# Winograd pairs of the up-projection: three PSUM tiles for one pair, weight sums loaded earlier, cache copies moved to the gate panels, residual updates at high priority

## The chip, the core and the metric

The kernel runs on one core of a Trainium2 chip. Such a core has five engines that run side by side, each through its own queue in program order: TensorE (PE in the profile; its weight loads are shown apart as PEld), VectorE (DVE), ScalarE (ACT), GpSimd (POOL) and SyncE (SP). Matmuls write to PSUM, which has eight banks of 2 KB per partition; the other data lies in SBUF. DMA transfers are issued by SyncE and, where they add to what lies in SBUF or copy from DRAM to DRAM, by GpSimd. Engines wait for each other through semaphores. The metric is the device time of one execution in microseconds.

## The reference

One layer of a hybrid decoder for 512 prompt tokens and 8 sample tokens, 520 columns in all, of width 1024. What this document speaks of comes behind the two attentions:

```
u = rmsnorm(x);  qA..gB = split(u @ w_in)
oA = dilated window attention;  oB = gated linear attention
mix = sigmoid(gA) * (oA @ w_pa) + sigmoid(gB) * (oB @ w_pb)
h = x + mix @ w_o
y = h + square(relu(rmsnorm(h) @ w_up)) @ w_down      # w_up 1024 x 4096
```

The sample group's key and value caches are copied to the outputs as well, some 40 MB.

## The kernel before

**Numbers.** Everything is fp32. Each operand is split into a high part (rounded to the matmul's fp32r format) and the rest, and a product takes three matmuls: high x high, high x low, low x high. The activations are kept transposed, 128 rows of the width by 520 columns (two halves of 260); `hh`/`hl` are the two parts of the residual times the norm's weight, `fh`/`fl` those of the squared Relu, `whi`/`wlo` those of the weights.

**Panels.** The weights come as a list of panels of 128 output columns (eight tiles of 128 x 128, 512 KB): 16 gate panels (`gA`, `gB`) end the input projection, then 2 for w_pa, 8 for w_pb, 8 for w_o, and four quarters of the feed-forward part. A plain panel (`panel_mm`) is 48 matmuls. SyncE loads panels two ahead into three rotating buffers (`raw`); ScalarE makes `whi` and VectorE `wlo` (`split_piece`, L107 and L108), half a panel at a time, for small panels in four rotating pairs of buffers.

**Pairs.** In the first three quarters two panels of w_up are done together (`pair_mm`, L185) in Winograd's form of a 2 x 2 block product, with seven products of 4 x 3 = 12 matmuls, where plain panels take eight. The three accumulators are x, e and a. P1 goes to x; ScalarE copies x to a (L1091); P5 goes to e; P6 is added to x, P3 to e, P7 to x, P2 to a, P4 to x. In between ScalarE and VectorE take copies and sums of what stands there (`up_pair`). a and e are the two banks of one PSUM tile, x is a bank of a second pool with four. At a pair's end come Relu, square and the split into `fh`/`fl`, which the eight panels of w_down then use; the fourth quarter uses plain panels.

**Sums.** Of the activations, the kernel forms `tr`, `Th`, `Tl` from the scaled residual `hg` (`column_sums`, L1064 to L1072), one k tile behind the residual update. Of the weights, `load_pair` loads the second panel into a tile `sums` (SyncE), and then GpSimd issues a DMA that adds parts of both panels onto it (L96); VectorE adds two more times (`s`, L122 and L123). There are three buffers for `sums`. A pair's loads are issued two panels ahead.

**Order.** The queues are filled by a scheduler that simulates the program and takes what is ready by priority; `high_priority` puts instructions ahead of others. `behind` fixes an order between two instructions of a queue, and all panel loads are chained so. `pace(1)` issues one of 42 copies of the caches (1 MB each) from GpSimd, behind the last matmul issued; before, it was called once per panel of w_pb, w_o and the feed-forward part, and once per pair.

Of the kernel before, what the change touches and what calls it, by code (L numbers as in the profile page):

```python
# [9 lines left out]
F32 = mybir.dt.float32  # L10
# [3 lines left out]
ALU = mybir.AluOpType  # L14
# [11 lines left out]
KT = 8  # L26
# [4 lines left out]
AHEAD = 4  # L31

# [15 lines left out]
class Build:  # L48
# [42 lines left out]
    def load_pair(self, i):  # L91

        ap, p = self.panels[i][0], self.late
        sums = p.tile([P, KT, P], F32, tag="sums", name="sums", bufs=3)
        self.load(sums, ap[1])
        self.nc.gpsimd.dma_start(sums.rearrange("p (i k) n -> p i (k n)", i=2),  # L96
                                 ap[:, :, :4].rearrange("i p k n -> p i (k n)"), accum_op=ALU.add)
        ra = self.raw_tile(KT)
        self.load(ra, ap[0])
        rb = p.tile([P, 4, P], F32, tag="rb", name="rb", bufs=2)  # L100
        self.load(rb, ap[1][:, 4:])
        self.raw[i] = (ra, rb, sums)
# [12 lines left out]
    def pair_pieces(self, i):  # L115
# [7 lines left out]
        nc.vector.tensor_tensor(s[:, 4:], s[:, :4], ra[:, 4:], op=ALU.add)  # L123
        both = self.split_piece(s, 0, KT)
# [3 lines left out]
        yield self.split_piece(ra, 4, 4)  # L128
# [36 lines left out]
    def start_panels(self, panels):  # L165
        self.panels, self.raw, self.split, self.wdst, self.cur, self.pieces = panels, {}, {}, {}, 0, {}
        self.jobs, self.ready = {}, {}

    def pair_mm(self, acts, done):
# [3 lines left out]
        ae, x = self.pm.tile([P, 2, 512], F32, tag="m", name="mps"), self.bank("mps")[:, :HC]  # L173
        a, e = (ae[:, j, :HC] for j in range(2))
        for q, (n, o, fresh) in enumerate((("P1", x, True), ("P5", e, True), ("P6", x, False), ("P3", e, False),
                                           ("P7", x, False), ("P2", a, False), ("P4", x, False))):
# [12 lines left out]
            done(n, ae, x)  # L189
# [5 lines left out]
    def panel_mms(self, xh, xl, m, pool=None):  # L195
# [3 lines left out]
        self.cur += 1  # L199
        if i + 2 < len(self.panels):  # L200
            self.load_panel(i + 2)
# [872 lines left out]
    def up_pair(self, p, work, k, fh, fl):  # L1074
# [12 lines left out]
        def done(n, ae, x):  # L1087
            a, e = (ae[:, j, :HC] for j in range(2))
# [9 lines left out]
            elif n == "P3":  # L1098
                nc.vector.tensor_tensor(e, e, v["P6"], op=ALU.add)
# [4 lines left out]
            elif n == "P2":  # L1104
                f = work()
# [3 lines left out]
                nc.scalar.activation(v["t"][:, two], v["t"][:, two], AF.Relu, scale=-1.0)  # L1109
            else:  # L1110
                t = v["t"]
# [457 lines left out]
```

## Time and profile before

| what | us |
|---|---|
| median of 3 runs (918.6 to 919.86) | 918.89 |
| the profiled execution | 918.5 |
| its span in the trace | 916.7 |
| w_o panels end, first pair starts | 528.87 |
| last pair ends, w_down of the third quarter starts | 768 |

The page's second part cuts the span into 40 slices of 22.9 us. The busy share of TensorE and VectorE is given in tenths, with the clock granted to TensorE in tenths of full speed and the mean busy share of the DMA engines:

```profile
PE   9999999999999999999999979999999999999996
DVE  6866656865868678677655666635763575556644
PEclk9999999999999999999999979999999999999999
DMA  7576465325543642221887984589658962222402
```

TensorE is full but for one slice (504 to 527 is the 23rd, 527 to 550 the 24th) and the end. The same slice has a lower clock. The DMA engines are busiest from the 20th slice (435 us) on and nearly free in the three slices ahead of it, where the gate panels run.

In the list of waits each row names who waited for whom, with the total in us, how often, and the longest. In the chain each row is a start, a duration and what ran; the chain follows what ended last back to the start. In the order of time a row's bracket gives the idle time ahead of it and what ended that. In the rows by stretch come the stretch, the busy us of PE, PEld, DVE, ACT and POOL (number of instructions), the granted clock, the DMA share and GB/s.

### The profile page before, as it was taken

How to read it: one execution, taken by the hardware profiler on the slowest of the kernel's cores; microseconds unless marked ns; L12 is line 12 of the kernel's file. 1: busy time of each engine (PE TensorE's matmuls, PEld its weight loads, DVE VectorE, ACT ScalarE, POOL GpSimd, SP SyncE). 2: the span in 40 equal slices, each digit the busy share in tenths (PEclk: the TensorE clock that was granted, in tenths of full speed). 3: DMA queues.
4: the chain of work that ended last, by engine and by line, in shares of the span. 5: the costliest groups of instructions: out<-in, count | busy, mean ns of one | idle time of the engine just before them, and what ended most of it. 6: DMA issues, size and time to landing. Idle time of an engine off the chain costs nothing.

```text
span 916.7 us, 19479 instructions
## 1 busy us (share of the span) xinstructions
PE 889.3 (97%) x8010; PEld 868.3 (95%) x8010; DVE 595.0 (65%) x1167; ACT 412.8 (45%) x832; POOL 87.7 (10%) x139
## 2 busy tenths in 40 slices
PE   9999999999999999999999979999999999999996
PEld 9999999999999999999999968899999999999996
DVE  6866656865868678677655666635763575556644
ACT  6334333444545453547334446623752374223442
POOL 1200000000111212010000210011001100000000
PEclk9999999999999999999999979999999999999999
DMA  7576465325543642221887984589658962222402
GB/s 250 157 236 208 139 204 192 117 74 166 183 155 128 208 166 72 76 93 53 310 311 275 304 260 150 207 280 349 221 212 295 359 192 93 93 93 91 140 7 88
DMA packets 42721, 165.16 MB, mean 180 GB/s; under 512 B 5692, under 2 KB 10820, under 8 KB 40808
## 3 DMA queue, kind: packets, MB, share of 16 engines
q1 hardware_dynamic: 33976, 97.93, 30.9%
q0 software_dynamic: 8368, 65.49, 21.2%
q8 instruction: 63, 1.03, 0.4%
q10 hardware_dynamic: 288, 0.49, 0.2%
q14 instruction: 26, 0.21, 0.1%
HBM read 150.17 MB, written 54.17 MB: 223 GB/s over the span
## 4 chain that ended last, share of the span: by engine, by line
PE 90%; ACT 4%; DMA 3%; DVE 2%; issue 1%; SPq 0%; DVEq 0%; ACTq 0%; POOLq 0%
PE mps L220 64%; PE mps L185 10%; PE mps L1384 5%; DMA sums<-in_w_up 2%; ACT whi L107 1%; PE mps L384 1%; PE lev L813 1%; PE sps L559 1%; PE pvp L592 1%; PE gpo L922 1%; PE gpu L926 1%; PE ptp L576 1%; PE vps L523 1%; PE gpo L924 1%; PE gso L994 0%
## 5 line engine op out<-in xcount | busy, mean ns | idle before, releaser
L107 ACT ACTIVATE whi<-raw 128x512 fp32r<-128x512 f32 (+1 forms) x242 | 149.6, 622 | 298.0 <-PE mps L220 247.0
L220 PE MATMUL mps<-uh,whi 128*128 128x260 f32 x896 | 255.8, 286 | 0.0
L220 PE MATMUL mps<-ul,whi 128*128 128x260 f32 x896 | 255.7, 285 | 0.0
L220 PE MATMUL mps<-uh,wlo 128*128 128x260 f32 x896 | 255.2, 285 | 0.0
L108 DVE TENSOR_TENSOR wlo<-raw,whi 128x512 fp32r<-128x512 f32 (+1 forms) x242 | 163.9, 680 | 75.5 <-ACT whi L107 73.2
L220 PEld LDWEIGHTS mps<-uh,wlo 128*128 128x128 f32 x896 | 168.7, 188 | 2.1 <-issue 1.3
L220 PEld LDWEIGHTS mps<-ul,whi 128*128 128x128 f32 x896 | 168.6, 188 | 1.2 <-issue 0.3
L220 PEld LDWEIGHTS mps<-uh,whi 128*128 128x128 f32 x896 | 168.7, 188 | 1.1 <-issue 0.7
L220 PE MATMUL mps<-fl,whi 128*128 128x260 f32 x384 | 108.2, 282 | 0.6 <-DVE fl L1085 0.6
L220 PE MATMUL mps<-fh,wlo 128*128 128x260 f32 x384 | 108.5, 283 | 0.0
L220 PE MATMUL mps<-fh,whi 128*128 128x260 f32 x384 | 108.5, 283 | 0.0
L220 PEld LDWEIGHTS mps<-fl,whi 128*128 128x128 f32 x384 | 72.2, 188 | 0.8 <-DVE fl L1085 0.8
L220 PEld LDWEIGHTS mps<-fh,whi 128*128 128x128 f32 x384 | 72.3, 188 | 0.0
L220 PEld LDWEIGHTS mps<-fh,wlo 128*128 128x128 f32 x384 | 72.2, 188 | 0.0
L185 PE MATMUL mps<-Th,whi 128*128 128x260 f32 x192 | 56.7, 295 | 15.6 <-ACT mps L1091 11.5
L185 PE MATMUL mps<-Tl,whi 128*128 128x260 f32 x192 | 55.4, 288 | 1.6 <-DVE Tl L1072 1.6
L185 PE MATMUL mps<-Th,wlo 128*128 128x260 f32 x192 | 54.9, 286 | 0.0
L185 PEld LDWEIGHTS mps<-Th,whi 128*128 128x128 f32 x192 | 36.8, 192 | 18.7 <-ACT mps L1091 14.2
L1384 PE MATMUL mps<-fh,lw 128*128 128x280 f32 (+1 forms) x256 | 46.8, 284 | 0.0
L185 PE MATMUL mps<-hl,whi 128*128 128x260 f32 x144 | 41.2, 286 | 0.0
L185 PE MATMUL mps<-hh,whi 128*128 128x260 f32 x144 | 41.2, 286 | 0.0
L185 PE MATMUL mps<-hh,wlo 128*128 128x260 f32 x144 | 41.1, 286 | 0.0
(381 smaller groups left out, 1921.1 us busy)
## 6 DMA issues: line engine op xcount, KB each, us to landing
raw<-in_w_in SPq DMA_DIRECT2D x55, 512.0 KB, 4.4
raw<-in_w_down SPq DMA_DIRECT2D x32, 512.0 KB, 3.3
raw<-in_w_up SPq DMA_DIRECT2D x20, 512.0 KB, 7.5
sums<-in_w_up SPq DMA_DIRECT2D x12, 512.0 KB, 8.8
sums<-in_w_up POOLq DMA_DIRECT2D x12, 512.0 KB, 9.7
sx<-in_state SPq DMA_DIRECT2D x8, 512.0 KB, 4.4
sx<-dV SPq DMA_DIRECT2D x8, 512.0 KB, 4.8
out_sgla<-sx POOLq DMA_DIRECT2D x8, 512.0 KB, 5.1
```

The source lines that it names most:

```text
L107: self.piece = (nc.scalar.activation(hi, raw[:, x:x + n], AF.Copy), nc.vector.tensor_tensor(lo, raw[:, x:x + n], hi.bitcast(F32), op=ALU.s ...
L108: nc.vector.tensor_tensor(lo, raw[:, x:x + n], hi.bitcast(F32), op=ALU.subtract))
L185: mm = nc.tensor.matmul(o, w[:, k], u, start=(fresh and k == 0 and y == 0), stop=(k == 3 and y == 2), skip_group_check=True)
L220: mm = self.nc.tensor.matmul(o[:, :HC], wt, x[:, k, j * HC:(j + 1) * HC], start=(k == 0 and n == 0), stop=(k == kt - 1 and n == 2))
L384: self.last = nc.tensor.matmul(ps[i][:, j, :HC], wt, u[:, k, j * HC:(j + 1) * HC], start=(k == 0 and n == 0), stop=(k == KT - 1 and n == 1))
L523: nc.tensor.transpose(pt[:, r * P:(r + 1) * P], vt[:, r * P:(r + 1) * P], self.c["ident"])
L559: m = nc.tensor.matmul(pss[hh][:, hp, c], Q[rows, i, b * P:(b + 1) * P], K[rows, i, ks], start=True, stop=True)
L576: nc.tensor.transpose(pt[:, hh, x], prs[hp][:, hh, x * P:(x + 1) * P], self.c["ident"])
L592: m = nc.tensor.matmul(po[64 * hh:64 * hh + 64, hp * P:(hp + 1) * P], v, pTs[hp][:, hh, x], start=(x == first), stop=(x == 1))
L813: m = self.nc.tensor.matmul(out, w, x, start=True, stop=True)
L922: nc.tensor.matmul(po[:, :256], ST[:, c], V[:, c], start=True, stop=(c == 0))
L1384: nc.tensor.matmul(ps, w, u[:, kk, cc], start=(kk == 0 and x == 0), stop=(kk == KT - 1 and x == 2))
```

## The change

Six edits:

- `pair_mm`: e is a tile of its own in the first pool, a and x are two banks of the second. P3's sum on VectorE goes to a work tile in SBUF instead of back to e, so that Relu on ScalarE handles a alone (260 columns) and the square on VectorE takes max(f, 0) x f.
- `load_sums`: the two DMAs of `sums` are issued up to 22 us of panel time ahead (10.04 per pair, 5.74 per panel), the raw parts of a pair as before.
- In the first pair, P2 is moved from the sixth to the third place and its weights are split earlier.
- `proj_scaled` issues one cache copy per gate panel, 16 in all; so the copies end in the first quarter's w_down instead of the third's.
- The residual update (`H`, `hh`, `hl`) is at high priority.
- `column_sums` of a k tile comes right behind its residual update.

```diff
+LEAD = 22.0
...
     def load_pair(self, i):
-        ap, p = self.panels[i][0], self.late
-        sums = p.tile([P, KT, P], F32, tag="sums", name="sums", bufs=3)
-        self.load(sums, ap[1])
-        self.nc.gpsimd.dma_start(sums.rearrange("p (i k) n -> p i (k n)", i=2),
-                                 ap[:, :, :4].rearrange("i p k n -> p i (k n)"), accum_op=ALU.add)
...
-        self.raw[i] = (ra, rb, sums)
+        self.raw[i] = (ra, rb, self.sums.pop(i))
+
+    def load_sums(self, i):
+        for j in range(i, len(self.panels)):
+            if self.at[j] - self.at[i] > LEAD:
+                return
+            if self.panels[j][1] == PAIR and j not in self.begun:
+                self.begun.add(j)
+                ap = self.panels[j][0]
+                self.sums[j] = t = self.late.tile([P, KT, P], F32, tag="sums", name="sums", bufs=3)
+                self.load(t, ap[1])
+                self.nc.gpsimd.dma_start(t.rearrange("p (i k) n -> p i (k n)", i=2),
+                                         ap[:, :, :4].rearrange("i p k n -> p i (k n)"), accum_op=ALU.add)
...
     def pair_mm(self, acts, done):
-        ae, x = self.pm.tile([P, 2, 512], F32, tag="m", name="mps"), self.bank("mps")[:, :HC]
-        a, e = (ae[:, j, :HC] for j in range(2))
+        self.load_sums(i)
+        e = self.pm.tile([P, 2, 512], F32, tag="m", name="mps")[:, 0, :HC]
+        a, x = (self.bank("mps")[:, :HC] for _ in range(2))
...
+        if i == self.first_pair:
+            seq.insert(2, seq.pop(5))
...
     def panel_mms(self, xh, xl, m, pool=None):
+        if self.late is not None:
+            self.load_sums(i)
...
-    def proj_scaled(self, dst):
+    def proj_scaled(self, dst, copies=0):
...
             self.fill(self.rate)
+            self.pace(copies)
...
             elif n == "P3":
-                nc.vector.tensor_tensor(e, e, v["P6"], op=ALU.add)
+                v["f"] = work()
+                nc.vector.tensor_tensor(v["f"][:, two], e, v["P6"], op=ALU.add)
...
-                nc.scalar.activation(halves(f), ae[:, :, :HC], AF.Relu)
-                nc.vector.tensor_tensor(f, f, f, op=ALU.mult)
+                nc.scalar.activation(f[:, one], a, AF.Relu)
+                nc.vector.scalar_tensor_tensor(f, f, 0.0, f, op0=ALU.max, op1=ALU.mult)
...
+                with tc.high_priority():
+                    nc.vector.tensor_tensor(halves(H[:, k]), ps, halves(H[:, k]), op=ALU.add)
...
-                if k > 0:
-                    self.column_sums(p, hg, k - 1, Th, Tl)
+                self.column_sums(p, hg, k, Th, Tl)
                 self.pace(1)
-            self.column_sums(p, hg, KT - 1, Th, Tl)
```

What stands in the queues moves with it. On SyncE, from the third w_o panel's load to the second pair's loads, before:

```order
L81 DMA raw<-in_w_o 128x1024 x6
L81 DMA sums<-in_w_up 128x1024
L81 DMA raw<-in_w_up 128x1024
L81 DMA rb<-in_w_up 128x512
L81 DMA sums<-in_w_up 128x1024
```

and in the changed program:

```order
L82 DMA raw<-in_w_o 128x1024 x5
L82 DMA sums<-in_w_up 128x1024
L82 DMA raw<-in_w_o 128x1024
L82 DMA sums<-in_w_up 128x1024
L82 DMA raw<-in_w_up 128x1024
L82 DMA rb<-in_w_up 128x512
```

The first `sums` has moved ahead of the last w_o panel's load, and the second ahead of the first pair's own panels.

On VectorE, beside the fifth to seventh w_o panel, behind the residual part `hl` of the fifth, before:

```order
L1302 SCALAR_TENSOR_TENSOR hl<-H,gcols,hh 128x520
L1067 TENSOR_TENSOR tr<-hg 128x260
L1068 SCALAR_TENSOR_TENSOR tr<-tr,hg 128x260
L1069 SCALAR_TENSOR_TENSOR tr<-tr,hg 128x260
L108 TENSOR_TENSOR wlo<-raw,whi 128x512
L1072 TENSOR_TENSOR Tl<-tr,Th 128x780
L122 TENSOR_TENSOR s<-sums,raw 128x512
L1300 TENSOR_TENSOR H<-mps,H 128x520
```

and in the changed program:

```order
L1327 SCALAR_TENSOR_TENSOR hl<-H,gcols,hh 128x520
L1088 TENSOR_TENSOR tr<-hg 128x260
L1089 SCALAR_TENSOR_TENSOR tr<-tr,hg 128x260
L132 TENSOR_TENSOR s<-sums,raw 128x512
L118 TENSOR_TENSOR wlo<-raw,whi 128x512
L1090 SCALAR_TENSOR_TENSOR tr<-tr,hg 128x260
L133 TENSOR_TENSOR s<-s,raw 128x512
L1325 TENSOR_TENSOR H<-mps,H 128x520
```

`s`, which waits for the sums, has moved ahead of `wlo`, the first half of the seventh w_o panel's weights.

On ScalarE, at the end of the second quarter's first pair, before (`t<-t 128x520` is the square of the pair's second output, `mps<-mps` the copy of x to a in the next pair):

```order
L1106 ACTIVATE t<-mps 128x520
L107 ACTIVATE whi<-raw 128x512
L1112 ACTIVATE t<-mps 128x260
L1113 ACTIVATE t<-t 128x520
L107 ACTIVATE whi<-rb 128x512
L1091 ACTIVATE mps<-mps 128x260
L1084 ACTIVATE fh<-t 128x520 x2
```

and in the changed program:

```order
L1129 ACTIVATE t<-mps 128x260
L117 ACTIVATE whi<-raw 128x512
L1135 ACTIVATE t<-mps 128x260
L1105 ACTIVATE fh<-t 128x520
L1136 ACTIVATE t<-t 128x520
L117 ACTIVATE whi<-rb 128x512
L1111 ACTIVATE mps<-mps 128x260
L1105 ACTIVATE fh<-t 128x520
```

One of the two `fh`, that of the pair's first output, has moved ahead of the copy.

More of the change, by code (lines that the diff above doesn't have):

```diff
@@ L166, in start_panels @@
         self.panels, self.raw, self.split, self.wdst, self.cur, self.pieces = panels, {}, {}, {}, 0, {}
-        self.jobs, self.ready = {}, {}
+        self.jobs, self.ready, self.sums, self.begun = {}, {}, {}, set()
+        self.at = np.cumsum([0.0] + [10.04 if p[1] == PAIR else 5.74 for p in panels])
     def pair_mm(self, acts, done):
@@ L188, in pair_mm @@
                     self.last = mm
-            done(n, ae, x)
+            done(n, a, e, x)
     def panel_mm(self, xh, xl, pool=None):
@@ L1085, in split, with done @@
             nc.vector.tensor_tensor(fl[:, k + x], f, fh[:, k + x].bitcast(F32), op=ALU.subtract)
-        def done(n, ae, x):
-            a, e = (ae[:, j, :HC] for j in range(2))
+        def done(n, a, e, x):
             if n == "P1":
@@ L1134, in run @@
         order += [(I["w_o"][i], KT) for i in range(8)]
+        self.first_pair = len(order)
         for qd in range(4):
```

32 lines of the change are left out of this document (19 added, 13 removed).

## The prediction

> **What bounds the kernel now.** I read the page's busy table first, then the waits of TensorE, then the chain, and last the order of time on each engine around the places where TensorE stops.
>
> ```profile
> span 916.7 us, 19479 instructions
> PE 889.3 (97%) x8010; PEld 868.3 (95%) x8010; DVE 595.0 (65%) x1167; ACT 412.8 (45%) x832; POOL 87.7 (10%) x139
> 768.15 91.84 PE mps L220 x768
> ```
>
> TensorE is the bound: it is idle for 916.7 - 889.3 = 27.4 us only. The third row is a stretch of the chain without a wait: 768 matmuls of 260 columns in 91.84 us, 0.1196 us each. That pitch is the measure for everything below: a plain panel of 48 matmuls should take 5.74 us, a pair of 84 (seven products of 12) 10.05 us. No edit takes a matmul away, so only idle time and slow clock can be won.
>
> ```profile
> PE mps L185 <- ACT mps L1091: 11.5, 12, 1.3
> PE mps L185 <- ACT Th L1071: 4.0, 2, 3.6
> PE mps L185 <- DVE Tl L1072: 1.6, 2, 1.2
> PE mps L220 <- DVE fl L1085: 0.6, 1, 0.6
> DVE s L122 <- DMA sums<-in_w_up: 16.9, 4, 5.7
>   issue: 4.1, 3
> ```
>
> These are waits: total us, how often, the longest. Four of them stop TensorE, all inside the pairs (L185) or right behind them; the rest of the idle time lies at the two ends of the program, which the change doesn't touch. The first is product P5 of each of the 12 pairs, which waits for ScalarE's copy of P1. The fifth row is VectorE, blocked on the weight sums that the second and third rows go back to; the last, from the view of the tile s, is idle time of VectorE ahead of s, 4.1 us more, for which the profile shows no releaser.
>
> **The change part by part.** *Separate tiles for a, e and x.* The restarts of P5, from the chain:
>
> ```profile
> 553.05 7.35 PE mps L185 x59
> 564.30 7.35 PE mps L185 x59
> 575.91 7.35 PE mps L185 x59
> 656.45 7.34 PE mps L185 x59
> 668.08 8.88 PE mps L185 x72
> ```
>
> From restart to restart a pair takes 11.25 us (564.30 - 553.05) or 11.6 us (575.91 - 564.30, 668.08 - 656.45). Against 10.05 us that is 1.19 or 1.57 us lost. Of the eleven pairs after the first, four are of the long kind (restarts at 553.05, 575.91, 668.08 and the last) and seven short: 4 x 1.57 + 7 x 1.19 = 14.6 us. In one of them the four small matmuls of the norm hide (about 0.5 us), so 14.1 us can go. With a tile of its own P5 needs nothing from the copy; P6 does, as it goes on in the bank that the copy reads. P5 covers 12 x 0.1196 = 1.44 us. What is late next is therefore the copy itself, behind what stands ahead of it on ScalarE:
>
> ```profile
> 550.79 0.37 ACT L1112 ACTIVATE t<-mps 128x260 f32<-128x260 f32 x1
> 551.05 0.63 ACT L1084 ACTIVATE fh<-t 128x520 fp32r<-128x520 f32 x1
> 551.59 0.62 ACT L1113 ACTIVATE t<-t 128x520 f32<-128x520 f32 x1
> 552.11 0.61 ACT L107 ACTIVATE whi<-rb 128x512 fp32r<-128x512 f32 x1
> 552.63 0.37 ACT L1091 ACTIVATE mps<-mps 128x260 f32<-128x260 f32 x1
> 550.17 0.28 PE L185 MATMUL mps<-hh,whi 128*128 128x260 f32 x1
> ```
>
> This is a long one: with fh ahead of it the copy ends 553.00 - 550.17 = 2.83 us behind the pair's first matmul, and P6 would want to start after 2 x 1.44 = 2.87 us. The changed order puts fh ahead of the copy in nearly every pair, so nearly all look like this one: just covered, with 0.04 us to spare. But fh waits for VectorE's square, and on VectorE a weight split (0.69 us, as s below) may stand ahead of that. I let a part of it through, 0.05 to 0.25 us, and take **0.12 us per pair, 1.3 us** in all; bounds 0 and, if the whole 0.69 less the 0.04 shows in some nine pairs, 6 us.
>
> *The half-width Relu and the fused max.* ScalarE's Relu goes from 520 to 260 columns, VectorE's square becomes a two-operation form (0.76 us, as hl below, for 0.69). Both lie beside TensorE: ScalarE is 45% and VectorE 65% busy. Nothing, between -0.1 and +0.1 us a pair, inside the 0.12 above.
>
> *Sums loaded earlier, residual at highest priority, P2 drawn ahead: the first pair.*
>
> ```profile
> 528.87 0.28 PE L185 MATMUL mps<-hh,whi 128*128 128x260 f32 x1
> 537.44 0.58 PE L185 MATMUL mps<-Th,whi 128*128 128x260 f32 x1 [3.63 <-ACT Th L1071]
> 514.95 0.43 DVE L1069 SCALAR_TENSOR_TENSOR tr<-tr,hg 128x260 f32<-128x260 f32 x1
> 520.78 0.69 DVE L122 TENSOR_TENSOR s<-sums,raw 128x512 f32<-128x512 f32 x1 [3.51 <-DMA sums<-in_w_up]
> 531.41 0.69 DVE L122 TENSOR_TENSOR s<-sums,raw 128x512 f32<-128x512 f32 x1 [2.60 <-DMA sums<-in_w_up]
> 534.57 0.70 DVE L1300 TENSOR_TENSOR H<-mps,H 128x520 f32<-128x520 f32 x1
> 536.71 0.76 DVE L1302 SCALAR_TENSOR_TENSOR hl<-H,gcols,hh 128x520 fp32r<-128x520 f32 x1
> 540.42 0.97 DVE L1072 TENSOR_TENSOR Tl<-tr,Th 128x780 fp32r<-128x780 f32 x1 [0.32 <-ACT Th L1071]
> 540.00:545.00 5.00, 4.16 (x18) 3.85 (x18) 1.12 (x3) 1.11 (x3) 0.50 (x1) 0.50 0.72 242
> ```
>
> The first pair runs from 528.87 to 550.17 (quoted above), 21.30 us, **11.25 over**: 1.1 us for the copy, 5.6 us of waits for Th and Tl (4.0 + 1.6 in the table above), and 4.5 us for the rest. In the last row, a stretch of 5 us, the third number from the end is the granted clock, 0.50: these 5 us alone lose 2.5, so I put the clock at 3 us and the restarts behind the waits at 1.5. VectorE stood still 3.51 and 2.60 us for the sums, so the last residual panel, finished on TensorE at 528.87, was added only at 534.57. From there to the end of the last Tl it took 541.39 - 534.57 = 6.8 us. If nothing blocks, that addition starts near 529.1, and Tl ends near 535.9; the changed order has two more weight splits in between (0.6 us apart), so 535.9 to 537.2. P6, now fourth, reaches its last quarter at 528.87 + 3 x 1.44 + 10 x 0.12 = 534.4. That leaves 1.5 to 2.8 us of waiting, plus 0.3 us for P2 behind the copy.
>
> Do the sums come early enough?
>
> ```profile
> 502.07 3.17 SPq L81 DMA_DIRECT2D sums<-in_w_up  x1
> 507.44 0.33 SPq L81 DMA_DIRECT2D raw<-in_w_up  x1
> 509.99 1.28 POOL L96 DMA_DIRECT2D sums<-in_w_up  x1 [3.14 <-ACT Th L1071]
> sums<-in_w_up POOLq DMA_DIRECT2D x1, 512.0 KB, 10.8
> raw<-in_w_up SPq DMA_DIRECT2D x1, 512.0 KB, 9.2
> 515.00:520.00 5.00, 5.00 (x44) 5.00 (x43) 1.98 (x3) 1.77 (x3) 0.00 (x0) 1.00 1.37 424
> ```
>
> Load issued at 502.07, adding DMA at 509.99, landed 10.8 us later. In the new queue of SyncE the first load stands one w_o panel (5.74 us) earlier, so it should be added by about 515; the other operand, the raw panel issued at 507.44, lands 9.2 us later, at 516.6, and does not move. In the changed order of VectorE this s stands ahead of the weight split of the seventh w_o panel, which TensorE wants at 517.4. That start is 528.87 less two panels. VectorE would be blocked from 514.95, where the work ahead of it ended (the row of tr), to 516.6 and the split end 0.3 to 0.7 us late: a new wait of **0.7 us** (0 to 3). The second sums gain about 6 us on 531.41 and are wanted near 522.5; the DMA engines are full there (share 1.37 in the last row), so I add 1 us. The first pair then keeps **4.0 us** of its 11.25 (1.5 to 8).
>
> The clock fell behind the wait of 3.63 us and not behind the others, of which the longest lasted 1.3 us; two waits of 1 to 2 us should leave it whole. [...]
>
> *16 cache copies beside the gate panels.* They go to POOL between steps of the gated attention.
>
> ```profile
> 360.00:380.00 20.00, 20.00 (x212) 19.39 (x202) 11.20 (x27) 7.51 (x20) 2.83 (x7) 1.00 0.24 87
> 362.23 1.64 POOL L916 COPY ST<-sd 32x128 f32<-32x128 f32 x4 [5.87 <-DVE sd L912]
> 366.60 0.59 PE L922 MATMUL gpo<-Vb,ST 128*128 128x256 f32 x2
> raw<-in_w_o SPq DMA_DIRECT2D x8, 512.0 KB, 7.2
> ```
>
> The DMA share is 0.24 there, and a panel beside copies lands after 7.2 us (w_o) while two panels, 11.5 us, are loaded ahead. A copy waits for its panel's end and holds POOL for that time; behind it stand the ST copies, done 366.60 - 363.87 = 2.7 us before they are needed. I take nothing (0 to 3 us). No gain either: TensorE waits for nothing there, and the w_o panels keep one copy each.
>
> **Sum.** To be won: 11.25 + 14.1 + 0.6 (fl) = 26.0 us. Kept: 4.0 + 0.7 + 1.3 and half of fl's wait, 0.3, as squares of the residual still stand ahead of it = 6.3. Won: 19.7 us. The profiled execution took 918.5 us (span 916.7), 0.4 below the median of the runs: 918.5 - 19.7 = 898.8, and on the median's scale about **899 us**.
>
> **Rivals.**
> - *The sums come no earlier,* because the DMA engines are full between 505 and 530 and not the queue is late. The first pair then loses all but the 1.1 us of the copy: 899 + (10.2 - 4.0) = 905. For it: the share of 1.37. Against it: the bytes up to then are the same, only their order differs.
> - *One wait in the first pair passes the 3.6 us* that took the clock before: 1.5 us more of waiting and 3 us of half clock, 903.5. For it: the sums may be late. Against it: the two waits that I expect lie apart. [...]
> - *The wait moves from P5 to P6,* since fh and the square hold the copy, or P5 stays tied to it: the pairs keep most of their loss, 899 + 11 x 1.07 = 911. Against it: the long kind above, covered with fh in place.
> - *Slower.* The adding DMAs still land late, and now everything passes on: VectorE's s holds the square, that holds fh, that the copy, that P6, and in the w_o panels s holds the weight split. VectorE stood still 16.9 and 4.1 us ahead of s before. If all 21 us reached TensorE, 899 + 21 = 920, and with one loss of clock 923. It decides from about 20 us passed on. Against it: most of these waits are to shrink, as no copy is left beside the pairs of the second and third quarter.
>
> **Chances.** Forecast 0.65, late sums 0.13, clock 0.10, P6 0.07, slower 0.05 (of it 0.02 within 0.2%). So faster 0.95, same 0.02, slower 0.03; 0.2% (1.8 us) is about what a measurement of this kernel tells from no change. The forecast's own bounds are 894.5 (the first pair keeps 1.5, nothing else: 918.5 - 26.0 + 1.5, on the median's scale) and 903; the range goes to 906.5 for the late sums and leaves out the last two cases.
>
> **What would show it.** Right: the wait of L1091's matmuls gone from 11.5 us to under 2, pairs 10.1 to 10.3 us apart, the first pair 13 to 15 us long, the clock 1.00 between 530 and 560, s no longer waiting for sums. Wrong: a wait of P6 for the copy of a microsecond per pair, VectorE blocked at s ahead of the seventh w_o panel, or idle TensorE beside the gate panels.

## The result and the profile after

The changed kernel takes **908.0 us** (median of four runs, 903.79 to 909.36), the kernel before, beside it, 918.75. The ratio is 0.9873 with a 95% interval of 0.9837 to 0.991. It is faster by 10.7 us, little more than half of what was forecast, and 908.0 lies outside the predicted range of 894.5 to 906.5. The profiled execution took 906.7 us (span 904.9). The two kernels' line numbers differ by some 20: L1111 is the copy that was L1091, L203 and L240 are the matmuls of pairs and plain panels.

The table of TensorE's waits, changed kernel (total in us, times, longest):

```profile
PE mps L240 <- DVE gA L1072: 3.8, 1, 3.8
PE mps L203 <- ACT Th L1092: 1.5, 1, 1.5
PE mps L203 <- DVE t L1124: 1.0, 1, 1.0
PE mps L203 <- DVE Tl L1093: 0.6, 1, 0.6
PE mps L203 <- ACT mps L1111: 0.4, 1, 0.4
```

The largest wait of before, 11.5 us in 12 pieces for the copy, is down to 0.4. A wait that was not there is now at the top: 3.8 us for the eviction of a gate panel. The starts of the first two pairs, and of w_down behind the fourth, in TensorE's timeline:

```profile
534.22 0.28 PE L203 MATMUL mps<-hh,whi 128*128 128x260 f32 x1
550.42 0.28 PE L203 MATMUL mps<-hh,whi 128*128 128x260 f32 x1
...
581.00 0.28 PE L240 MATMUL mps<-fh,whi 128*128 128x260 f32 x1
```

The first pair began at 528.87 before and begins at 534.22 now: **5.35 us are lost ahead of all pairs.** It lasts 16.20 us (21.30 before), and the three behind it (581.00 - 550.42) / 3 = 10.19 us each. Of the 5.35 us, 3.8 are the wait for gA; behind it the matmuls run at half pace for 3 us (346.48 to 349.5), which is another 1.5. How the wait came about, as it stands in the chain of work that ended last, cut to the stretch 318 to 348 us (start, us, what):

```profile
323.78 0.34 DVE vs L993
324.12 0.02 issue
324.13 4.26 DMA dV<-vs
...
328.84 11.23 DMA sx<-dV
340.07 0.02 issue
340.09 0.52 ACT sx L1020
...
343.87 1.19 DVE sx L1021 x3
345.05 0.60 DVE wlo L118
345.65 0.08 DVE el L857
345.73 0.61 DVE gA L1072
346.35 0.14 issue
346.48 1.64 PE mps L240 x6
```

It reads from TensorE backwards: the matmul at 346.48 waits for a PSUM tile, which VectorE empties at 345.73 (gA), behind its work on `sx`; that waits for a 512 KB load that took 11.23 us, and this for the 8 KB of `dV`, which took 4.26. (`sx` belongs to the gated attention of the samples, which runs between the gate panels. Its new values go through DRAM: `vs` is stored to `dV`, and `sx` is loaded from there, spread over all partitions.) The same stretch in windows (length, then busy time of PE, PEld, DVE, ACT, POOL; the third number from the end is the granted clock, the next the share of the DMA engines), and a stretch of the first pair:

```profile
340.00:345.00 5.00, 2.72 (x23) 2.51 (x22) 4.70 (x11) 4.91 (x12) 1.31 (x2) 1.00 1.20 419
345.00:350.00 5.00, 3.52 (x18) 3.55 (x19) 5.00 (x14) 2.07 (x6) 4.58 (x2) 0.66 0.58 192
...
545.00:550.00 5.00, 4.01 (x24) 3.80 (x23) 4.37 (x8) 2.75 (x4) 0.00 (x0) 0.74 1.05 324
```

Behind each set of waits the clock falls for some microseconds, to 0.66 and to 0.74 of these stretches.

### The profile page after: what moved, and what is told of

Its sections match the earlier page's. It is cut to its first block, busy times and chain, and to the rows that moved or that the text cites. A ratio compares the mean times of both kernels' runs of the same rounds, so it can differ in the third digit from the quotient of the medians.

```text
span 904.9 us, 19492 instructions
## 1 busy us (share of the span) xinstructions
PE 887.8 (98%) x8010; PEld 868.5 (96%) x8010; DVE 594.7 (66%) x1167; ACT 409.6 (45%) x832; POOL 88.8 (10%) x139
## 4 chain that ended last, share of the span: by engine, by line
PE 94%; DMA 2%; DVE 2%; ACT 1%; issue 0%; SPq 0%; DVEq 0%; ACTq 0%
PE mps L240 65%; PE mps L203 13%; PE mps L1407 5%; DMA sx<-dV 1%; PE lev L833 1%; PE mps L404 1%; PE sps L579 1%; PE pvp L612 1%; PE gpo L942 1%; PE gpu L946 1%; PE ptp L596 1%; PE vps L543 1%; PE gpo L944 1%; DMA dV<-vs 0%; DMA xr<-in_xT 0%
## 5 line engine op out<-in xcount | busy, mean ns | idle before, releaser
L240 PE MATMUL mps<-uh,whi 128*128 128x260 f32 x896 | 256.6, 286 | 3.8 <-DVE gA L1072 3.8
L240 PE MATMUL mps<-ul,whi 128*128 128x260 f32 x896 | 256.6, 286 | 0.0
L240 PE MATMUL mps<-uh,wlo 128*128 128x260 f32 x896 | 255.7, 286 | 0.0
L240 PEld LDWEIGHTS mps<-uh,whi 128*128 128x128 f32 x896 | 169.3, 189 | 5.0 <-ACT D L894 3.9
L240 PEld LDWEIGHTS mps<-uh,wlo 128*128 128x128 f32 x896 | 169.4, 189 | 2.1 <-issue 1.5
L240 PEld LDWEIGHTS mps<-ul,whi 128*128 128x128 f32 x896 | 169.4, 189 | 1.2 <-issue 0.3
L240 PE MATMUL mps<-fh,wlo 128*128 128x260 f32 x384 | 108.5, 283 | 0.0
L240 PE MATMUL mps<-fh,whi 128*128 128x260 f32 x384 | 108.5, 282 | 0.0
L240 PE MATMUL mps<-fl,whi 128*128 128x260 f32 x384 | 108.2, 282 | 0.2 <-DVE fl L1106 0.2
L240 PEld LDWEIGHTS mps<-fl,whi 128*128 128x128 f32 x384 | 72.2, 188 | 0.4 <-DVE fl L1106 0.4
L240 PEld LDWEIGHTS mps<-fh,whi 128*128 128x128 f32 x384 | 72.3, 188 | 0.0
L240 PEld LDWEIGHTS mps<-fh,wlo 128*128 128x128 f32 x384 | 72.2, 188 | 0.0
L203 PE MATMUL mps<-Th,whi 128*128 128x260 f32 x192 | 56.3, 293 | 2.6 <-ACT Th L1092 1.5
L203 PE MATMUL mps<-Tl,whi 128*128 128x260 f32 x192 | 54.8, 285 | 0.6 <-DVE Tl L1093 0.6
L203 PE MATMUL mps<-Th,wlo 128*128 128x260 f32 x192 | 54.6, 284 | 0.0
L203 PE MATMUL mps<-hh,whi 128*128 128x260 f32 x144 | 40.9, 284 | 0.4 <-ACT mps L1111 0.4
L203 PE MATMUL mps<-hh,wlo 128*128 128x260 f32 x144 | 40.9, 284 | 0.0
L203 PE MATMUL mps<-hl,whi 128*128 128x260 f32 x144 | 40.8, 283 | 0.0
L203 PEld LDWEIGHTS mps<-Th,whi 128*128 128x128 f32 x192 | 36.7, 191 | 4.0 <-ACT Th L1092 1.7
```

The costliest lines, as they stand in the source:

```text
L203: mm = nc.tensor.matmul(o, w[:, k], u, start=(fresh and k == 0 and y == 0), stop=(k == 3 and y == 2), skip_group_check=True)
L240: mm = self.nc.tensor.matmul(o[:, :HC], wt, x[:, k, j * HC:(j + 1) * HC], start=(k == 0 and n == 0), stop=(k == kt - 1 and n == 2))
```

## The experiments

Two questions: what the 16 copies beside the gate panels cost and win, and what the other parts are worth. Medians in us; each ratio is against runs of the kernel before on the same chip, whose medians lie between 918.4 and 919.5 (917.5 for the last run).

| run | time | ratio, 95% interval |
|---|---|---|
| the change | 908.0 | 0.9873 (0.9837-0.9910) |
| change, no gate copies | 913.8 | 0.9941 (0.9920-0.9962) |
| change, 4 KB stubs at the gate | 914.8 | 0.9952 (0.9936-0.9968) |
| change, VectorE's order held | 907.6 | 0.9876 (0.9860-0.9892) |
| before + gate copies | 921.5 | 1.0027 (1.0010-1.0044) |
| change, 16 copies at gB | 908.9 | 0.9890 (0.9859-0.9921) |
| change, copies late | 914.5 | 0.9962 (0.9941-0.9982) |
| before + tiles | 916.5 | 0.9974 (0.9953-0.9995) |
| change, residual plain | 907.9 | 0.9867 (0.9837-0.9898) |
| change, copies placed | 904.3 | 0.9839 (0.9819-0.9858) |
| placed + P3 ahead | 904.7 | 0.9847 (0.9827-0.9867) |
| change, lead of two panels | 910.1 | 0.9902 (0.9885-0.9919) |
| before + tiles + gate copies | 909.0 | 0.9893 (0.9866-0.9920) |
| placed, residual plain | 902.5 | 0.9814 (0.9795-0.9833) |
| placed, lead of two panels | 908.1 | 0.9878 (0.9860-0.9895) |
| placed, P2 late | 903.8 | 0.9831 (0.9812-0.9850) |
| placed, one tile again | 918.2 | 0.9993 (0.9977-1.0009) |
| placed, residual plain, splits held | 900.5 | 0.9804 (0.9783-0.9825) |

**No copies beside the gate panels.**

```diff
-        self.proj_scaled(gA, 1)
+        self.proj_scaled(gA)
-        self.proj_scaled(gB, 1)
+        self.proj_scaled(gB)
```

> The changed kernel without the 16 cache copies beside the gate panels; they follow one place later each, beside w_pb, w_o, the pairs and w_down, as before the change. Theory D (the copies' bytes slow the broadcast load of sx, ScalarE and VectorE stand at sx, the gA eviction comes late): sx<-dV lands in 4 to 7 us (11.2 after the change), no TensorE wait for gA, the w_o panels end at 529 and not at 534.2, time 902 to 904. Rival P (the copies hold GpSimd's queue) says the same. Rival R (the 5 us are lost for another reason, the pieces drawn early): stays at 907 to 909.

All three missed the time: the wait for gA is gone and the w_o panels end at 529.51, as D and P had it (`sx` lands after 7.2 us), yet the kernel is 6 us slower than the change ((0.9941 - 0.9873) x 919). In the second pair of the second quarter, and again of the third, 5 us are lost. The chain of that run at the first of these places:

```profile
608.89 18.50 DMA sums<-in_w_up
...
627.99 4.21 DMA sums<-in_w_up
632.20 0.61 DVE wlo L118
632.81 3.57 issue
636.38 0.06 DVE s L132
...
637.59 0.70 DVE t L1130
638.29 0.02 issue
638.31 0.02 ACT fh L1105
...
639.90 0.38 ACT mps L1111
640.28 0.04 issue
640.32 4.71 PE mps L203 x26
```

The load of the weight sums takes 18.5 us beside the copies, so the adding DMA is issued late, at 627.99. It lands 8.3 us later, at 636.3, and s starts then; for the 3.57 us that VectorE stands the chain itself names no releaser. Behind s stand the square t and ScalarE's fh, and behind these the copy for which P6 waits. It is the mechanism of the prediction's rival "slower", with two of the stalls in place of all. In the changed kernel, whose copies are gone by then, s waited 0.4 us for sums in all:

```profile
DMA sums<-in_w_up: 0.4, 1
```

**The same 16 instructions without their bytes,** 4 KB each; the rest of each copy follows later.

```diff
-            self.pace(copies)
+            if copies:
+                o, i = self.copies[k]
+                self.copies[k:k + 1] = [(o[:, 64:], i[:, 64:])]
+                self.copies.insert(0, (o[:, :64], i[:, :64]))
+                self.pace(1)
```

> The 16 copies beside the gate panels cut to their first 64 columns (4 KB each instead of 1 MB); the rest of each follows at the later places. The same 16 instructions stand in GpSimd's queue with the same waits, only the bytes are gone. Theory D: as without copies, sx<-dV in 4 to 7 us, no TensorE wait for gA, 902 to 904. Rival P (GpSimd's queue held by the copies' waits): the wait of 3.8 us stays, 907 to 909.

No wait for gA, so GpSimd's queue is not the cause. The time of 902 to 904 was missed for the reason just shown: the two stalls are here too. The eight last additions on `sx` (L1021) start from 336.8 to 344.6 us in the changed kernel and from 331.3 to 335.1 with the stubs.

What all profiles share is the time that `dV` takes, from its issue on SyncE to the issue of the loads that wait for it (changed kernel, then stubs):

```profile
324.13 0.29 SPq L994 DMA_DIRECT2D dV<-vs  x1
328.47 0.80 SPq L1006 DMA_DIRECT2D sx<-dV  x2
...
324.29 0.29 SPq L994 DMA_DIRECT2D dV<-vs  x1
325.67 0.80 SPq L1006 DMA_DIRECT2D sx<-dV  x2
```

It is 4.32 to 4.47 us in all six profiles with copies of 1 MB beside gA and 1.37 to 1.39 in the other thirteen. The load of `sx` is less regular: 6.0, 7.2, 7.5, 7.7, 7.7 and 11.2 us with the copies, 5.6 to 7.3 without. So the chain starts 3 us later each time, and how much of it reaches TensorE depends on that load too.

**The copies with their bytes, VectorE's order as without them.** The scheduler counts a copy's bytes, so the copies had also moved the gA evictions behind `sx` and `kl`. Here they were tied back by order alone:

```diff
+ORDER = [('sx3.2', 'ev.10'), ('ev.10', 'sx3.3'), ('sx3.7', 'ls.2'), ('ev.11', 'kl.2')]
...
+        for a, b in ORDER:
+            if key in (a, b) and a in self.handles and b in self.handles:
+                self.behind(self.handles[b], self.handles[a])
```

(`sx3.n` are the last head's additions, `ev.10` and `ev.11` the third and fourth gA evictions, `ls.2` and `kl.2` the steps of D and kl.)

> All 16 copies with their bytes, but VectorE's order around the last head's sx held as it is without copies (sx ahead of the third gA eviction and of D, the fourth gA eviction ahead of kl). Theory D: sx<-dV still takes 9 to 12 us, VectorE stands at sx with the gA eviction behind it, TensorE still waits 2 to 6 us for gA, 905 to 910. Rival O (only the new order of VectorE puts the eviction late): TensorE waits for no gA, 902 to 904.

907.6: TensorE waits 1.2 us for gA and 2.7 for gB, and the w_o panels end at 535.85. The wait moves in part, the loss stays, so the order alone is not it. With the stubs this leaves the bytes as the cause. Theory D's own figure failed, though: `sx` landed after 7.7 us and not 9 to 12, and what was late was `dV` (4.36).

**The copies alone on the kernel before.**

```diff
             self.fill(self.rate)
+            self.pace(copies)
...
-        self.proj_scaled(gA)
+        self.proj_scaled(gA, 1)
-        self.proj_scaled(gB)
+        self.proj_scaled(gB, 1)
```

> The kernel before with nothing changed but the 16 copies beside the gate panels. Theory D: the gate panels lose the same 5.3 us, w_o ends near 534, and nothing is won for it: 923 to 925, or 920 to 923 if fewer copies beside the pairs give back some of it. Rival R (the loss needs the rest of the change): 917 to 919.

921.5, slower by 2.5 us, theory D in its second form: the gate loses 3.2 us in that profile (w_o ends at 532.04, 528.87 before; a wait of 2.2 us for gA), and little comes back.

**All 16 beside gB.**

```diff
-        self.proj_scaled(gA, 1)
+        self.proj_scaled(gA)
-        self.proj_scaled(gB, 1)
+        self.proj_scaled(gB, 2)
```

> The changed kernel with its 16 copies all beside the gB panels, two each, and none beside gA: no copy is under way while the last sx is loaded, and as many copies as in the changed kernel are gone when the pairs begin. Theory D (bytes beside the load of sx cost the 5.3 us at gA; copies beside the pairs cost two stalls of 5 us each, as the run without gate copies showed): sx<-dV lands in 4 to 7 us, TensorE waits for no gA, the w_o panels end near 529 to 531, the pairs of the second and third quarter run as after the change, 902 to 905. Rival B (16 copies in half the time load the DMA engines so that gB, or the w_pb panels, come late): a wait of 2 to 5 us there, 905 to 909.

The time is rival B's. The wait for gA is gone, and two stalls stand beside the gB panels, in the gated attention of the last head:

```profile
PE lev L833 <- issue: 3.5, 1, 3.5
PE gpo L942 <- POOL ST L936: 2.9, 1, 2.9
```

For the first of them the profile shows no releaser. The DMA engines are full there (a share of 1.04 from 390 to 400 and 1.05 from 400 to 410, 0.32 and 0.15 before), but how that reaches TensorE was not tried; and this execution took 913.76, 4.9 us above the median, so its stalls are not those of a usual one.

**No copies until the second half.**

```diff
                 split(1, t)
-                self.pace(1)
...
-                    self.pace(1)
+                    self.pace((0, 1 if k < 4 else 0, 1)[qd])
...
-                    self.pace(1)
+                    self.pace(2 if k % 2 else 1)
```

(The gate calls are as in the run without gate copies.)

> No copies beside the gate panels and none beside the pairs or the w_down panels of the first quarter; one beside each of the first four w_down panels of the second quarter, one beside each of the third, three for two w_up panels of the fourth, the rest at its end. Theory S (copies cost where an adding DMA or sx is waited for, and nothing where no load is late): no wait at gA, no stall of 5 us in the second and third quarter, 901 to 904. Rival E (too many bytes at the end: late w_up or w_down panels of the fourth quarter, or the last copies end behind the last output): 906 to 915, with waits for raw panels behind 765 us or a span that ends with a copy.

Rival E in its first form. The pairs' stalls are gone and the third w_down ends at 797.56 (809.25 without gate copies), but the last w_down's first half takes 34.92 us in place of 24.96 before, from its first matmul to the second half's: there ScalarE waits 10.6 us for weights that load beside the copies.

**The tiles alone on the kernel before:** the three tiles, the half-width Relu and the fused max.

```diff
-        ae, x = self.pm.tile([P, 2, 512], F32, tag="m", name="mps"), self.bank("mps")[:, :HC]
-        a, e = (ae[:, j, :HC] for j in range(2))
+        e = self.pm.tile([P, 2, 512], F32, tag="m", name="mps")[:, 0, :HC]
+        a, x = (self.bank("mps")[:, :HC] for _ in range(2))
```

> The kernel before with the pair's three PSUM banks as separate tiles and the half-width Relu alone; sums, copies, residual and the order of P2 as before. If the tiles remove what they removed in the changed kernel (waits of the copy 11.5 to under 2 us, 14.1 to 2.6 us with the restarts): 918.9 - 11.5 = 907. Rival S (late sums now pass from VectorE to fh, the copy and P6, as in the run without gate copies): one or two stalls of 3 to 5 us remain in the second and third quarter, 911 to 917. In both the first pair keeps about its 11 us, or 1 less.

916.5: rival S. The table of waits, of an execution 3.8 us above that median, has for the copy:

```profile
PE mps L185 <- ACT mps L1090: 10.0, 4, 4.5
```

Twelve waits of 1 us have become four, of up to 4.5 us, now in the second and third pairs of the second and third quarter, with the same chain through sums, s, square and fh.

**The residual at plain priority.**

```diff
-                with tc.high_priority():
-                    nc.vector.tensor_tensor(halves(H[:, k]), ps, halves(H[:, k]), op=ALU.add)
+                nc.vector.tensor_tensor(halves(H[:, k]), ps, halves(H[:, k]), op=ALU.add)
```

(The next two instructions likewise.)

> The changed kernel with the residual's additions and splits at plain priority again. If the priority does what the change says: the last addition of the residual starts later than 1.0 us behind the last w_o panel, Th and Tl come 1 to 3 us later, the first pair takes 17 to 20 us (16.2 after the change), 909 to 912. Rival (the earlier sums alone did it): VectorE's order there stays nearly the same, the first pair 16 to 16.5 us, 907 to 909.

907.9, no different. In the two traces VectorE, ScalarE, GpSimd and SyncE run the same instructions in the same order, so here the priority changes nothing, and the run is the change measured a second time. All the same its profile has a first pair of 20.2 us (16.2) and a wait for gA of 1.2 (3.8): that much two profiles of one order can differ.

**The copies placed by what had been learnt:** none beside gA, one per gB panel, none beside the pairs and the first w_down, the rest beside the later w_down and w_up panels.

```diff
-        self.proj_scaled(gA, 1)
+        self.proj_scaled(gA)
...
                 split(1, t)
-                self.pace(1)
...
-                    self.pace(1)
+                    self.pace((0, 1 if k < 4 else 0, 1)[qd])
```

> The changed kernel with its copies placed by what the runs showed: none beside gA, one beside each gB panel, w_pb and w_o as they are, none beside the pairs and the w_down panels of the first quarter, one beside each of the first four w_down panels of the second, all eight of the third, and the first six w_up panels of the fourth. Theory S (copies cost only beside sx, beside the loads and adds of the sums, and in the last 50 us): w_o ends near 529, no stall in the pairs behind the first, the last stage as long as after the change, 901 to 904. Rival G (copies beside gB cost as well): w_o ends at 531 to 535, 905 to 909.

904.3: theory S in its signs, and just above its range in time. The w_o panels end at 529.74, no pair behind the first stalls, the last stage has its old length; the first pair now takes 18.1 us.

**P3 ahead of P6 in the first pair,** on the placed copies.

```diff
-            seq.insert(2, seq.pop(5))
+            seq[2:6] = seq[5], seq[3], seq[2], seq[4]
```

(P3's addition waits for P6's value, and the split of s gives P3's half first.)

> As the run with placed copies, and in the first pair P3, which takes its columns from hh and hl, is multiplied ahead of P6, the first product that needs the last Th and Tl. Theory V (the first pair keeps 6 us since VectorE needs 7.7 us from the last addition of the residual to Tl, and the waits of about 1 to 1.5 us that follow one another halve the clock): P6 starts 1.4 us later, the waits for Th and Tl shrink from 2.1 to about 0.7, the clock stays whole or loses less, the first pair takes 12 to 14 us (16.2 after the change) and the kernel is 2 to 4 us faster than with placed copies alone. Rival C (the clock is taken by the load on the engine, not by the waits): the first pair still shows half clock for 5 us and gains at most 1.4.

904.7, no gain: theory V missed. The first pair takes 18.4 us and the clock is at 0.50 from 544 to 549, as rival C foretold, but this doesn't decide for C either, as the waits did not shrink. That for Th went, others took its place (1.3 us for ScalarE's P, 2.3 for VectorE's t), 4.8 us in all where the placed copies had 4.5.

**The sums begun two panels ahead,** as before.

```diff
-            if self.at[j] - self.at[i] > LEAD:
+            if j - i > 2:
```

> The changed kernel with the weight sums begun two panels ahead, as before the change, and not 22 us ahead; everything else as changed. If the lead gives what it was given in the prediction: s waits for its sums again by 2 to 4 us in the last w_o panels, the first pair keeps 10 to 11 us of waiting and half clock (6.2 with the lead), 911 to 914. Rival T (the copies being gone from beside the pairs is what counts, the lead is spare): first pair 16 to 17 us, 907 to 909.

910.1, 2.7 us more, between the two forecasts. s waits 15.1 us for its sums again (0.4 with the lead), but the intervals of the times overlap, so it was made again without the stall at gA (below).

**Tiles and gate copies on the kernel before,** the two edits to it shown above together.

> The kernel before with two parts of the change: the separate tiles and the 16 copies beside the gate panels. Alone they gave 916.5 and 921.5 beside 918.4 to 919.1 before. If the two only add: 919. If the tiles pay only where no copies lie beside the pairs (theory S): the two stalls of 4 to 6 us in the second and third quarter go, the gate panels lose 2 to 5, the first pair keeps about 11: 910 to 914.

909.0. The tiles alone won 2.4 us (0.0026 x 919), the copies alone lost 2.5, the two together win 9.8: **the copies pay only with the tiles, and the tiles pay in full only with the copies moved.** The other four edits add 1.8 us to that (0.9873 against 0.9893), within the intervals.

**One part undone at a time, on the placed copies.** With neither stall present the parts can be told apart. First, two of the three banks in one tile again:

```diff
-        e = self.pm.tile([P, 2, 512], F32, tag="m", name="mps")[:, 0, :HC]
-        a, x = (self.bank("mps")[:, :HC] for _ in range(2))
+        ae, x = self.pm.tile([P, 2, 512], F32, tag="m", name="mps"), self.bank("mps")[:, :HC]
+        a, e = (ae[:, j, :HC] for j in range(2))
```

> The kernel with placed copies, two of the pair's three banks in one tile again (the copy into one of them waits for P5 in the other), all else as it is. If the tiles are worth what the prediction counted: the copy's waits come back, 11 to 14 us, 915 to 918. Rival (the tiles are worth only the 2 us that they gave alone, the rest was the copies): 905 to 908.

```profile
PE mps L203 <- ACT mps L1111: 16.6, 12, 4.6
```

918.2: the tiles are worth (0.9993 - 0.9839) x 919 = **14.2 us** here, and all twelve waits are back (this execution took 923.27, so their sum is above the usual one). Next the lead, `j - i > 2` as above:

> The kernel with placed copies, the weight sums begun two panels ahead as before the change. If the lead is worth the 2 us that 910.1 against 908.0 showed: 906 to 907, with a longer first pair and 1 us lost at w_down. If it is spare: 903.5 to 905.

908.1: the lead is worth 3.6 us ((0.9878 - 0.9839) x 919), more than expected, and s waits 14.5 us for its sums again (0.2 on the placed copies). Then the residual at plain priority, as above, and P2 back in its place:

```diff
-        if i == self.first_pair:
-            seq.insert(2, seq.pop(5))
```

> The kernel with placed copies (904.3 us, first pair 18.1 us long) with the residual at plain priority. If the priority wins what the first pair showed (16.2 us with it, 20.2 without, one profile each): 906 to 908 and a first pair of 20 to 22 us. If that difference was only the chance of the stall at gA ahead of it: 903.5 to 905.

> The kernel with placed copies, P2 of the first pair back in its sixth place. P6 then starts 1.4 us earlier and waits 1.4 us longer for Th: by that alone no change, 904 to 905; if one wait of about 2.5 to 3 us halves the clock for longer: 906 to 909.

902.5 and 903.8: neither the priority nor P2 drawn ahead wins anything. Here too the four engines run the same order with and without the priority, so 904.3 and 902.5 are two measurements of one order: 1.8 us is what such a pair can differ by, and the worth of P2 is not told from nothing. The sixth edit, `column_sums` right behind the residual update, was not undone alone.

**VectorE freed in the first pair:** residual plain, and the first two weight splits for the second pair tied behind the last Tl.

```diff
+            if i == self.first_pair + 1:
+                self.behind(self.piece[1], self.summed)
```

> Placed copies, residual at plain priority (902.5), and VectorE's first two weight splits for the second pair held behind the last Tl: 1.2 us of VectorE less ahead of it. Theory V (the first pair waits for VectorE's chain from the last addition of the residual to Tl): Th and Tl come about 1 us earlier, the waits for them shrink from 2.1 to about 1, the kernel takes 899 to 902. Rival A (ScalarE's hh, hg and Th set that chain, or the splits are then late themselves): 902 to 905.

900.5, the fastest of all, 0.9804 against 0.9814 without the tie, which by itself is within the intervals. The profile speaks for theory V, though: from the start of the last residual addition to the end of the last Tl it takes 6.77 us (7.68 to 7.70 in four profiles without the tie), and Th and Tl are waited for 0.6 us each (1.5 and 0.6 before). The first pair takes 14.4 us (532.01 to 546.38), and the clock stays whole, as in this window:

```profile
540.00:545.00 5.00, 3.52 (x27) 3.31 (x28) 4.07 (x8) 2.78 (x5) 1.22 (x1) 1.00 1.41 424
```

That the tie kept the clock is not shown: in the run with VectorE's order held the first pair takes 15.75 us with 4.6 us of waits, only 1.1 us beyond these and its 10.05 of matmuls, which leaves less than the 1.5 us that 3 us of half clock take.

## Why the prediction was wrong, step by step

Against its own scale, 898.8 for the profiled execution, the changed kernel's took 906.7: 7.9 us more. By its steps that is 5.35 at the gate, 2.15 in the first pair, 1.3 in the other pairs, less 0.7 for the seventh w_o panel and 0.1 for fl, together 8.0. The median lies another 1.3 us above the profiled run.

**The step that failed: "16 cache copies beside the gate panels ... I take nothing (0 to 3 us)".** It looked at GpSimd, which the copies hold, at the ST copies behind them, and at weight panels that land after 7.2 us and are loaded 11.5 us ahead. The stubs show that holding GpSimd costs nothing. It left out the loads that are *not* loaded ahead: dV and sx are a chain of two DMAs between two steps of one computation, with ScalarE's and VectorE's queues waiting at its end and the PSUM evictions behind them. The mean DMA share of 0.24, from 360 to 380, said nothing of the 16 us (324 to 340) in which this chain runs. In place of nothing the gate lost 5.35 us in the profile shown. The loss differs from profile to profile (TensorE's wait for gA in the six with copies beside gA: from none to 3.8 us). In medians, the placed copies are 3.1 us faster than the change, and 4.9 us in the second measurement of each (0.9867 - 0.9814); they also have fewer copies behind w_o, so not all of this need be the gate.

**"No gain either" failed too.** Its words were that TensorE waits for nothing there; the gain lies 250 us later. With the copies beside the gate none are left beside the pairs of the second and third quarter, and without that the freed copy waits for fh, behind late sums (7.6 us in all without gate copies, 10.0 with the tiles alone). The prediction used the absence of copies as an argument against its rival "slower", and did not see that this was what its 14.1 us hung on.

**The tiles: right,** with that condition. Forecast were 14.1 us less 1.3 kept, 12.8; undoing them costs 14.2. In the changed kernel the eleven later pairs lose 2.6 us together beyond 10.05 each, 2.1 of it without the four matmuls that form the norm: 0.19 us a pair where 0.12 was taken. In the third pair VectorE is not behind it: ScalarE works without a pause from 560.65 on, its copy ends at 563.41, P6 starts at 563.46, and the matmuls around that start are 0.20 and 0.22 us apart in place of 0.12.

**The first pair: mechanism right, size short.** Forecast 4.0 us (1.5 to 8), measured 6.15. The waits were nearly as told: 0.4 for the copy (0.3), 1.5 + 0.6 for Th and Tl (1.5 to 2.8). Not foreseen were 1.0 us for t, behind a 1.22 us weight split on VectorE, and 3.4 us of half clock (544.20 to 547.62). The sentence "two waits of 1 to 2 us should leave it whole" is the error; the rival on the clock named the effect, but made it depend on a single wait past 3.6 us, and the longest was 1.5.

**The lead of the sums: right,** worth 3.6 us on the placed copies. The rival "late sums" did not happen. **Residual at highest priority and P2 ahead: no gain shown,** though the forecast built the first pair's 4.0 us on an addition that starts at once. It starts 1.0 us behind the panel's end (535.25), though the priority was at its highest: VectorE is full long before, as the next paragraph shows. From the addition's start to the end of the last Tl it then takes 7.70 us, within the 6.8 to 8.1 of the forecast.

**The seventh w_o panel:** s stood there 1.73 us for its raw panel, as told, but TensorE did not wait in the w_o panels (0.7 forecast):

```profile
521.99 0.69 DVE L132 TENSOR_TENSOR s<-sums,raw 128x512 f32<-128x512 f32 x1 [1.73 <-DMA raw<-in_w_up]
```

The wait came out elsewhere. From this s on VectorE's rows show no wait up to 541.05, so what s waits moves the last residual addition with it. That addition starts 13.26 us behind s (521.99 to 535.25), and 13.25 to 13.28 us behind it in seven more profiles (placed copies: 517.69 to 530.95). In some profiles the second pair's s waits for its raw panel as well. Of the 12 profiles with the tiles and the lead of 22 us, five have s waits of 3.5 to 4.5 us in all, and their first pairs take 19.2 to 20.2 us; in the other seven the waits come to 1.7 to 2.4 us, and the first pairs take 14.4 to 18.4. The prediction priced the wait at s as a late weight split; the profiles show it as a term of the first pair.

## What to carry to other kernels

Before moving background copies into a quiet stretch, look for loads there that are issued only when their data is ready, and at who stands in order behind them: a mean DMA share hides them (0.24 here, from 360 to 380). A wait that is removed may have covered a later one, so ask what the freed instruction waits for next, and test two such edits together as well as alone. Add up the short waits of TensorE that lie close together, and do not look at the longest alone: in the changed kernel 1.83 us of idle time within 3.41 us (3.41 - 1.58), the longest wait 1.53 us, were followed by half clock. And measure one order of instructions twice before you give a part of 2 us to an edit: here two profiles of one order had first pairs of 16.2 and 20.2 us.

## What the runs showed of the hardware

**The clock fell behind several short waits.** In the first pairs the half clock came in stretches, most of them 2.8 to 3.7 us long by the spacing of the matmuls (0.22 us in place of 0.12; in the changed kernel from 544.20 to 547.62, 3.4 us). Cut by that length, from an edge of the half clock, the windows of three runs (changed kernel; placed copies; placed, residual plain) show the busy time that went ahead, the second number of each row:

```profile
537.38:540.79 3.41, 2.79 (x21) 2.57 (x21) 3.35 (x8) 2.60 (x6) 1.81 (x2) 1.00 0.34 117
540.79:544.20 3.41, 1.58 (x11) 1.39 (x11) 1.24 (x2) 1.24 (x2) 0.75 (x1) 0.99 0.97 260
544.20:547.61 3.41, 3.41 (x18) 3.41 (x17) 1.98 (x3) 1.70 (x2) 0.47 (x1) 0.51 1.43 481
```

```profile
535.53:538.94 3.41, 1.30 (x9) 0.89 (x8) 2.14 (x4) 1.27 (x3) 0.11 (x2) 0.99 0.85 265
538.94:542.35 3.41, 3.41 (x17) 3.41 (x17) 0.31 (x1) 0.99 (x2) 1.21 (x1) 0.51 1.65 481
542.35:545.76 3.41, 1.66 (x14) 1.45 (x13) 3.38 (x6) 2.04 (x4) 0.00 (x0) 0.99 0.46 107
```

```profile
533.84:537.25 3.41, 1.68 (x13) 1.68 (x14) 3.41 (x6) 3.13 (x8) 0.61 (x2) 1.00 0.81 121
537.25:540.66 3.41, 1.52 (x11) 1.11 (x9) 2.45 (x5) 1.75 (x3) 0.00 (x0) 1.00 1.02 382
540.66:544.07 3.41, 3.19 (x14) 3.19 (x15) 0.16 (x1) 0.39 (x1) 0.00 (x0) 0.50 0.85 344
544.07:547.48 3.41, 1.61 (x13) 1.41 (x12) 3.10 (x5) 2.22 (x3) 1.22 (x1) 1.00 0.37 47
```

In these three runs a stretch in which TensorE was busy for 1.3 to 1.58 us of 3.41 was followed by one at 0.5, one with 1.68 or more by full clock; the border is not sharp, since one with 1.66 (placed copies, 542.35 to 545.76) was followed by 0.50 (545.76 to 549.11) and one with 1.61 (residual plain, 544.07 to 547.48) by full clock. In the last of these runs a single wait of 3.2 us (3.48 from one matmul's start to the next, 532.09 to 535.57) took nothing: TensorE was busy for 1.94 us of the 3.41 up to 533.84 and for 1.68 of the next, and the clock is 1.00 until 540.66. So the idle sum of such a stretch fits these profiles better than the longest wait; why that is so was not shown, and no run tried it by itself. In three profiles with two stretches of half clock in the first pair these end 6.76 us (placed copies, 542.35 and 549.11), 6.79 us (change, residual plain; 544.62 and 551.41) and 6.81 us (placed, lead of two; 544.25 and 551.06) apart.

**Copies of 1 MB delayed a small transfer more than the panels.** Beside them the 8 KB of dV took 4.32 to 4.47 us in six profiles, against 1.37 to 1.39 in thirteen without; the 512 KB weight panels of the same stretch (315 to 350) landed after 5.7 to 6.4 us, against 3.3 to 3.8. The 512 KB load behind dV took 11.2 us in the changed kernel (7.3 before), with a DMA share of 1.08 from 329 to 335 (0.28 with the stubs), but 6.0 to 7.7 in the other five.
